# Running the first two token blocks in halves: where the head of an eight-core decoder kernel waits for its loads

## The chip, the cores and the metric

The kernel runs on all 8 cores of one Trainium2 chip. Every core handles one prompt sequence of 2048 tokens, as four blocks of 512, and 128 sample tokens as a fifth block, and reads all the weights for itself. The metric is the time of the slowest core in microseconds (us) on the device. Executions agree within about 0.3% when nothing disturbs them.

Two kinds of disturbed runs occur, whatever the kernel. In slow runs one die, or both, run at a lower granted clock (down to 0.81 here) and the time rises by 28 to 513 us; they are left out. Besides, in some runs one pair of neighbouring cores has a granted clock near 0.982 instead of 0.994, and takes about 27 us longer than the rest; these count as fast runs by the rule used, but 27 us is more than what this study is about. I call a run **clean** when no core is below 0.988, and give for each kernel the median of its clean runs. As a second measure I give the median span of all cores above 0.988, over all its runs.

## The reference, cut to what matters

Two layers. Each begins with half a step of a gated feed-forward network (FFN), then a token mixer, then another such half step and a gated embedding. The change touches the first FFN alone:

```python
def rmsnorm(x, g):
    inv = lax.rsqrt(jnp.mean(x * x, axis=-1, keepdims=True) + NORM_EPS)
    return x * inv * g
def swiglu(h, w_gate_up, w_down):
    gu = h @ w_gate_up                     # (B, S, 2*D_FF), D_FF = 2816 = 22 * 128
    gate, up = gu[..., :D_FF], gu[..., D_FF:]
    return (jax.nn.silu(gate) * up) @ w_down
x = x + 0.5 * swiglu(rmsnorm(x, norm_ffn[i, 0]), w_ffn_gate_up[i, 0], w_ffn_down[i, 0])
```

D_MODEL is 1024, so X of a block of 512 tokens is 8 chunks of 128 x 512 f32: 256 KB a chunk, 2 MB a block. A weight tile ("gu") holds 128 gate and 128 up columns: 1 MB in f32, written as 512 KB of bf16.

## The kernel before

X lies in SBUF, the core's working memory, with the features on its 128 partitions. A recording layer keeps the regions that every instruction reads and writes, and works out the semaphores that each has to wait for. Weights come through a ring, issued by GpSimd; X is issued by SyncE, and every second chunk of block 0 by ScalarE. One unit of the gate and up stage is one weight tile on one block: 16 matmuls of 512 columns, 3.45 us when TensorE runs at full clock. The first FFN starts with "lead" tiles: four tiles run on block 0, then block 1, while blocks 2 to 4 still load. For blocks 0 and 1 the norm's scale is applied after the matmuls, so that they can start on any chunk that has landed.

```python
# the recording layer: the region of an access pattern (X arenas have quads == False)
lo, hi = base + off * es, base + (off + ext) * es      # from the first element to the last
...
if not quads:
    return ((arena, lo, hi),)

# norm of blocks 0 and 1, chunk by chunk
class RawNorm:
    def chunk(self, c):
        dve_ts(H[b][:, c, :], X[b][:, c, :], pcol(self.gname, c), ALU.mult)      # VectorE
        act(sq[:, 0:n], X[b][:, c, :], AF.Square)                               # ScalarE
    def stats(self):        # sum of squares by 8 matmuls with ones, then 1/sqrt on ScalarE

# the loads at the start (cut)
W.pump(1)                                              # weight tile 0
dma("act", PAR[:, :], d_par[:, :], "psem")
for b in range(NB):
    for c in range(8):
        dma("act" if b == 0 and c % 2 else "sp", X[b][:, c, :], ..., f"x{b}_{c}",
            extra=(("wsem2", 0, 16),) if b == 1 and c == 0 else ())    # X1 after weight tile 1
W.extra[1] = (("x0_3", 0, 16),)                        # tiles 1 and 2 after chunk 3 of X0
W.extra[3] = (("x1_2", 0, 16),)                        # tile 3 after chunk 2 of X1
W.extra[4] = tuple((f"x{SB}_{c}", 0, 16) for c in range(8))   # tile 4 and later after X4
W.pump()
...
first = [(0, 0), (1, 0), (2, 0), (0, 1), (1, 1), (2, 1), (3, 0), (3, 1)]   # (tile, block)
advance(ffn(0, 0, "norm_mix0", lead=4, raw=raw, first=first, arrive=arrive))
```

A name such as `wsem2` stands for the landing of a weight tile: `wsem0` is tile 0, `wsem2` tile 1, `wsem8` tile 4. A wait of this sort on an issue is called a gate below.

## Time and profile before

| | before |
|---|---|
| time, median of 3 runs (4 later) | 2630.95 us (2631.64) |
| spans of the cores in the profiled run | 2617.4 to 2623.8 us, clock 0.994 to 0.995 |
| TensorE busy | 98% of the span |
| TensorE idle in the first 60 us of core 3 | 60 - 41.78 = 18.2 us |
| first matmul of block 2, core 3 | 55.45 us |

First the page: its head and the line with the busy time of each engine (engine, us, share of the span, instructions).

```profile
span 2623.8 us, 34956 instructions; the slowest of 8 cores (2617.4 to 2623.8 us)
PE 2569.3 (98%) x14375; PEld 1245.7 (47%) x14375; DVE 1154.5 (44%) x2039; ACT 708.4 (27%) x1257; POOL 168.0 (6%) x254
```

TensorE (PE) has 2569 us of matmuls, and no order removes one. Only its idle time is to be had. The windows view of core 3, the slowest core of this run, says where that lies: each line is one stretch, its length, then each engine's busy time and instructions, the granted clock, the DMA's busy share and GB/s.

```profile
0.00:60.00 60.00, 41.78 (x180) 17.38 (x181) 28.77 (x67) 35.25 (x53) 5.11 (x13) 1.00 0.85 203
60.00:110.00 50.00, 50.00 (x293) 25.18 (x292) 25.62 (x50) 14.05 (x30) 2.12 (x4) 1.00 0.49 84
110.00:500.00 390.00, 390.00 (x2076) 187.80 (x2074) 160.71 (x253) 63.56 (x112) 10.59 (x20) 1.00 0.18 30
```

All the idle time up to 500 us is in the first 60 us. The waits of TensorE up to 85 us (total, times, longest) and its timeline (start, duration, then what ended the idle time before) say what it waits for:

```profile
PE ps L553 <- DMA ring<-wts: 13.8, 3, 12.3
PE ps L553 <- DVE h_50 L523: 1.5, 1, 1.5
PE ps L553 <- DVE h_49 L528: 1.4, 2, 1.1
PE ps L553 <- ACT sq_88 L510: 1.4, 1, 1.4
```

```profile
12.29 5.55 PE L553 MATMUL ps<-h_48,ring 128*128 128x512 bf16 x16 [12.29 <-DMA ring<-wts]
17.68 1.89 PE L553 MATMUL ps<-hid_56,ones 128*128 128x512 bf16 x8
20.88 3.63 PE L553 MATMUL ps<-h_48,ring 128*128 128x512 bf16 x16 [1.31 <-DMA ring<-wts]
24.67 3.63 PE L553 MATMUL ps<-h_48,ring 128*128 128x512 bf16 x16 [0.17 <-DMA ring<-wts]
28.13 1.03 PE L553 MATMUL ps<-h_49,ring 128*128 128x512 bf16 x4
...
55.45 1.90 PE L553 MATMUL ps<-h_50,ring 128*128 128x512 bf16 x8 [1.53 <-DVE h_50 L523]
```

The names h_48 to h_52 are blocks 0 to 4, x_43 to x_47 their X. TensorE starts when tile 0 has landed, runs block 0 on tiles 0 to 2, then block 1 as its chunks come. Of the 18.2 us, 12.3 pass before the first matmul. The rest is in six small waits.

From 8 to 11 us, while all three queues had work, they moved almost the same number of packets, and the weights' packets took most of the time:

```profile
q0 software_dynamic: 74, 0.30, 61.8%
q1 hardware_dynamic: 75, 0.15, 18.1%
q10 hardware_dynamic: 77, 0.16, 16.7%
```

The MB of this view are bytes written: a weight tile counts as 0.52 MB, though 1 MB is read for it.

### The profile page before, as it was taken

The numbers are of one execution on the slowest core, as the hardware profiler recorded it, in microseconds if no ns is written. First come the engines' busy times: TensorE is split into PE (matmuls) and PEld (weight loads), VectorE is DVE, ScalarE is ACT, GpSimd is POOL, SyncE is SP. The second block draws the span as 40 slices with busy tenths as digits, with TensorE's granted clock in tenths as the row PEclk, the third lists the DMA queues.
The fourth block names the chain that finished last, engine by engine and source line by source line (L and its number), as shares of the span: only waits on it lengthen the run. The fifth ranks groups of instructions, "written<-read, shape, count | busy, mean of one in ns | idle before, by whom it ended". The sixth has DMA issues, their size and how long they took to land.

```text
span 2623.8 us, 34956 instructions; the slowest of 8 cores (2617.4 to 2623.8 us)
## 1 busy us (share of the span) xinstructions
PE 2569.3 (98%) x14375; PEld 1245.7 (47%) x14375; DVE 1154.5 (44%) x2039; ACT 708.4 (27%) x1257; POOL 168.0 (6%) x254
## 2 busy tenths in 40 slices
PE   7999999999899999999999999999999999999997
PEld 3544544444454454444444454445444544544443
DVE  5432344755632222258732222267667322222687
ACT  5210112336621001124521001123334210011254
POOL 0000000012300000000000000000005000000000
PEclk9999999999999999999999999999999999999998
DMA  8220321146341123112042031102310320322113
GB/s 199 51 45 1 65 45 25 24 100 120 78 74 33 25 39 54 29 29 50 1 77 41 17 57 33 33 13 42 61 33 8 57 53 17 57 37 41 21 22 137
DMA packets 53311, 127.18 MB, mean 48 GB/s; under 512 B 9504, under 2 KB 24608, under 8 KB 53024
## 3 DMA queue, kind: packets, MB, share of 16 engines
q0 software_dynamic: 23584, 92.55, 20.4%
q1 hardware_dynamic: 28848, 31.29, 4.4%
q8 instruction: 113, 1.85, 0.3%
q10 hardware_dynamic: 720, 1.11, 0.1%
q14 instruction: 46, 0.38, 0.0%
HBM read 196.61 MB, written 10.62 MB: 79 GB/s over the span
## 4 chain that ended last, share of the span: by engine, by line
PE 88%; DVE 5%; ACT 2%; DMA 2%; issue 1%; SPq 1%; POOL 0%; ACTq 0%; DVEq 0%; POOLq 0%
PE ps L553 88%; SPq L577 1%; DMA ring<-wts 1%; ACT L508 1%; DVE h_50 L523 1%; DVE x_46 L523 0%; DVE h_51 L523 0%; DMA x_43<-xT 0%; DMA rr<-u 0%; DVE h_48 L523 0%; DVE h_49 L523 0%; POOL scr_96 L519 0%; DVE x_45 L523 0%; DVE x_43 L523 0%; DVE scr_93 L523 0%
## 5 line engine op out<-in xcount | busy, mean ns | idle before, releaser
L553 PE MATMUL ps<-h_48,ring 128*128 128x512 bf16 x1892 | 429.6, 380 | 14.4 <-DMA ring<-wts 14.4
L553 PE MATMUL ps<-h_51,ring 128*128 128x512 bf16 x1892 | 427.8, 380 | 3.2 <-DVE scr_96 L523 3.0
L553 PE MATMUL ps<-h_49,ring 128*128 128x512 bf16 x1892 | 427.7, 379 | 1.9 <-DVE h_49 L528 1.4
L553 PE MATMUL ps<-h_50,ring 128*128 128x512 bf16 x1892 | 426.2, 379 | 1.5 <-DVE h_50 L523 1.5
L553 PEld LDWEIGHTS ps<-h_51,ring 128*128 128x128 bf16 x1892 | 185.0, 98 | 228.0 <-DVE scr_96 L523 4.0
L553 PEld LDWEIGHTS ps<-h_50,ring 128*128 128x128 bf16 x1892 | 184.7, 98 | 225.3 <-DVE h_50 L523 2.0
L553 PEld LDWEIGHTS ps<-h_49,ring 128*128 128x128 bf16 x1892 | 184.4, 98 | 225.0 <-DVE h_49 L528 3.8
L553 PEld LDWEIGHTS ps<-h_48,ring 128*128 128x128 bf16 x1892 | 181.4, 98 | 220.1 <-issue 14.6
L577 POOL DMA_DIRECT2D ring<-wts x152 | 80.8, 538 | 2048.6 <-PE ps L553 1960.7
L553 PE MATMUL ps<-hid_56,ring 128*128 128x512 bf16 x736 | 163.8, 379 | 0.0
L553 PE MATMUL ps<-hid_54,ring 128*128 128x512 bf16 x736 | 163.7, 379 | 0.0
L553 PE MATMUL ps<-hid_55,ring 128*128 128x512 bf16 x736 | 163.7, 379 | 0.0
L553 PE MATMUL ps<-hid_53,ring 128*128 128x512 bf16 x736 | 162.8, 379 | 0.0
L510 ACT ACTIVATE scr_94<-ps 128x512 f32<-128x512 f32 (+1 forms) x109 | 61.6, 565 | 323.2 <-PE ps L553 322.9
L510 ACT ACTIVATE scr_97<-ps 128x512 f32<-128x512 f32 (+1 forms) x134 | 69.8, 521 | 282.4 <-PE ps L553 274.8
L510 ACT ACTIVATE scr_96<-ps 128x512 f32<-128x512 f32 (+1 forms) x120 | 68.5, 571 | 237.4 <-PE ps L553 235.2
L510 ACT ACTIVATE scr_95<-ps 128x512 f32<-128x512 f32 (+1 forms) x131 | 68.6, 524 | 234.8 <-PE ps L553 234.5
L553 PE MATMUL ps<-h_52,ring 128*128 128x128 bf16 x1892 | 124.5, 221 | 4.6 <-DVE scr_95 L523 3.1
L553 PEld LDWEIGHTS ps<-h_52,ring 128*128 128x128 bf16 x1892 | 115.3, 99 | 27.5 <-DVE scr_95 L523 3.3
L553 PEld LDWEIGHTS ps<-hid_56,ring 128*128 128x128 bf16 x736 | 72.0, 98 | 86.8
L553 PEld LDWEIGHTS ps<-hid_54,ring 128*128 128x128 bf16 x736 | 72.0, 98 | 86.6
L553 PEld LDWEIGHTS ps<-hid_55,ring 128*128 128x128 bf16 x736 | 72.0, 98 | 86.6
(490 smaller groups left out, 2171.8 us busy)
## 6 DMA issues: line engine op xcount, KB each, us to landing
ring<-wts POOLq DMA_DIRECT2D x110, 512.0 KB, 8.4
ring<-wts POOLq DMA_DIRECT2D x40, 768.0 KB, 6.4
rr<-u SPq DMA_DIRECT2D x48, 135.0 KB, 5.3
rr<-u SPq DMA_DIRECT2D x16, 134.8 KB, 3.5
x_44<-xT SPq DMA_DIRECT2D x8, 256.0 KB, 6.2
x_45<-xT SPq DMA_DIRECT2D x8, 256.0 KB, 11.2
x_46<-xT SPq DMA_DIRECT2D x8, 256.0 KB, 11.6
yT<-x_43 SPq DMA_DIRECT2D x8, 256.0 KB, 2.1
```

The lines of the kernel that those rows point to most:

```text
L508: e.preload_act_table_set(tset)
L510: return e.activation(out=out, in_=in_, func=func, **kw)
L523: S.op("dve", lambda e: e.scalar_tensor_tensor(out=out, in0=in0, scalar=scalar, in1=in1, op0=op0, op1=op1), reads=rd, writes=[out])
L553: ins = e.matmul(o_, l, r, start=st, stop=sp)
L577: S.op(eng, lambda e: e.dma_start(out=out, in_=in_), reads=[in_], writes=[out], dma_sem=sem, dma_total=total, extra_deps=extra)
```

## The change

The intent: TensorE should start on 256 tokens of block 0 as soon as those have landed, and likewise in block 1; X of each half loads by itself; a fifth lead tile gives TensorE 6.9 us more work before block 2 is needed. The gates move from the weights to X: weight tiles 0 to 4 are issued at once, X0's second half after its first, X1 after tile 1, X2 and later after tile 4. Shortened:

```diff
-        def chunk(self, c):
+        def chunk(self, c, lo=0, hi=512):
...
-                ensure(("n" if rw is None else "raw", b))
+                for t in (("n", b),) if rw is None else (("raw", b, 0), ("raw", b, 1)):
+                    if not half or t[2] <= half[0]:
+                        ensure(t)
...
-    W.pump(1)
+    def load_x(eng, b, c0, c1, lo=0, hi=None, extra=()):
+        dma(eng, X[b][:, c0:c1, lo:hi], src[:, c0:c1, lo:hi], f"x{b}_{c0}_{lo}", extra=extra)   # (cut)
     dma("act", PAR[:, :], d_par[:, :], "psem")
-    for b in range(NB):
-        for c in range(8):
-            dma("act" if b == 0 and c % 2 else "sp", X[b][:, c, :], d_xT[:, o_:o_ + n], f"x{b}_{c}",
-                extra=(("wsem2", 0, 16),) if b == 1 and c == 0 else ())
-    W.extra[1] = (("x0_3", 0, 16),)
-    W.extra[3] = (("x1_2", 0, 16),)
-    W.extra[4] = tuple((f"x{SB}_{c}", 0, 16) for c in range(8))
+    for c in range(0, 8, 2):
+        load_x("sp", 0, c, c + 2, 0, 256)
+    for c in range(0, 8, 2):
+        load_x("act", 0, c, c + 2, 256, 512, (("x0_6_0", 0, 16),) if c == 0 else ())
+    for lo in (0, 256):
+        for c in (0, 4):
+            load_x("sp", 1, c, c + 4, lo, lo + 256, (("wsem2", 0, 16),) if lo + c == 0 else ())
+    for b in range(2, NB):
+        for c in range(0, 8, 2):
+            load_x("sp", b, c, c + 2, extra=(("wsem8", 0, 16),) if b == 2 and c == 0 else ())
+    W.extra[5] = tuple((f"x{SB}_{c}_0", 0, 16) for c in range(0, 8, 2))
     W.pump()
...
-    first = [(0, 0), (1, 0), (2, 0), (0, 1), (1, 1), (2, 1), (3, 0), (3, 1)]
-    advance(ffn(0, 0, "norm_mix0", lead=4, raw=raw, first=first, arrive=arrive))
+    first = [(0, 0, 0), (0, 0, 1), (1, 0), (2, 0), (0, 1, 0), (1, 1, 0), (2, 1, 0), (3, 0), (0, 1, 1), (1, 1, 1), (2, 1, 1)]
+    first += [(3, 1), (4, 0), (4, 1)]          # (tile, block, half)
+    advance(ffn(0, 0, "norm_mix0", lead=5, raw=raw, first=first, arrive=arrive))
```

A transfer of a half now covers two chunks (four in block 1) and 256 of the 512 columns of each.

More of the change, by code (lines that the diff above doesn't have):

```diff
@@ L735, in __init__, with stats @@
             self.rs = RSB[b]
-        def chunk(self, c):
-            n, b = self.n, self.b
-            sq = HID[SB - 1 - b][:, c, :]
-            dve_ts(H[b][:, c, :], X[b][:, c, :], pcol(self.gname, c), ALU.mult)
-            act(sq[:, 0:n], X[b][:, c, :], AF.Square)
-        def stats(self):
-            n = self.n
+        def chunk(self, c, lo=0, hi=512):
+            b = self.b
+            dve_ts(H[b][:, c, lo:hi], X[b][:, c, lo:hi], pcol(self.gname, c), ALU.mult)
+            act(HID[SB - 1 - b][:, c, lo:hi], X[b][:, c, lo:hi], AF.Square)
+        def stats(self, lo=0, hi=512):
             pb = bank()
-            mm(pb[:, 0:n], [(ONES[:, :], HID[SB - 1 - self.b][:, c, 0:n]) for c in range(8)])
-            act(self.rs[:, 0:n], pb[:, 0:n], AF.Abs_reciprocal_sqrt, bias=NORM_EPS)
+            mm(pb[:, lo:hi], [(ONES[:, :], HID[SB - 1 - self.b][:, c, lo:hi]) for c in range(8)])
+            act(self.rs[:, lo:hi], pb[:, lo:hi], AF.Abs_reciprocal_sqrt, bias=NORM_EPS)
             bfree(pb)
@@ L752, in lead_order @@
         for b in range(NB):
-            out += [(t, b) for t in range(min(lead, nt)) if (t, b) not in out]
+            out += [(t, b) for t in range(min(lead, nt)) if (t, b) not in [x[:2] for x in out]]
         for t in range(lead, nt):
@@ L756, in lead_order @@
         last = {}
-        for i, (t, b) in enumerate(out):
-            last[t] = i
+        for i, x in enumerate(out):
+            last[x[0]] = i
         return out, last
@@ L818, in ffn @@
             order, last = lead_order(len(part), lead if pi == 0 else 0, first if pi == 0 else None)
-            for oi, (j, b) in enumerate(order):
-                n = BLK[b]
+            for oi, (j, b, *half) in enumerate(order):
+                lo, hi = (256 * half[0], 256 * half[0] + 256) if half else (0, BLK[b])
+                n = hi - lo
                 rw = raw[b] if b < len(raw) else None
-                ensure(("n" if rw is None else "raw", b))
+                for t in (("n", b),) if rw is None else (("raw", b, 0), ("raw", b, 1)):
+                    if not half or t[2] <= half[0]:
+                        ensure(t)
                 key = ("gu", l, f, part[j])
@@ L825, in ffn, with tail @@
                 pg, pu = bank(), bank()
-                pe_t[0] = max(pe_t[0], arrive.get((pi, j, b), 0.0))
+                pe_t[0] = max(pe_t[0], arrive.get((pi, j, b, *half), 0.0))
                 if rw is not None and pi == 0 and j == 0:
                     for k in range(8):
-                        mm_ops([(pg[:, 0:n], wt[:, k, 0:128], H[b][:, k, :], k == 0, k == 7),
-                                (pu[:, 0:n], wt[:, k, 128:256], H[b][:, k, :], k == 0, k == 7)])
+                        mm_ops([(pg[:, 0:n], wt[:, k, 0:128], H[b][:, k, lo:hi], k == 0, k == 7),
+                                (pu[:, 0:n], wt[:, k, 128:256], H[b][:, k, lo:hi], k == 0, k == 7)])
                         pe_t[0] += 2 * (n + 6.5) / 2400.0
-                    rw.stats()
+                    rw.stats(lo, hi)
                 else:
-                    mm(pg[:, 0:n], [(wt[:, k, 0:128], H[b][:, k, :]) for k in range(8)])
-                    mm(pu[:, 0:n], [(wt[:, k, 128:256], H[b][:, k, :]) for k in range(8)])
+                    mm(pg[:, 0:n], [(wt[:, k, 0:128], H[b][:, k, lo:hi]) for k in range(8)])
+                    mm(pu[:, 0:n], [(wt[:, k, 128:256], H[b][:, k, lo:hi]) for k in range(8)])
                 sg = scr()
                 if rw is not None:
-                    dve_tt(sg[:, 0:n], pg[:, 0:n], rw.rs[:, 0:n], ALU.mult)
+                    rs = rw.rs[:, lo:hi]
+                    dve_tt(sg[:, 0:n], pg[:, 0:n], rs, ALU.mult)
                     bfree(pg)
                     act(sg[:, 0:n], sg[:, 0:n], AF.Silu)
-                    def tail(b=b, j=j, n=n, sg=sg, pu=pu, rs=rw.rs):
-                        dve_tt(sg[:, 0:n], sg[:, 0:n], rs[:, 0:n], ALU.mult)
-                        dve_tt(HID[b][:, j, :], pu[:, 0:n], sg[:, 0:n], ALU.mult)
+                    def tail(b=b, j=j, n=n, lo=lo, hi=hi, sg=sg, pu=pu, rs=rs):
+                        dve_tt(sg[:, 0:n], sg[:, 0:n], rs, ALU.mult)
+                        dve_tt(HID[b][:, j, lo:hi], pu[:, 0:n], sg[:, 0:n], ALU.mult)
                         bfree(pu)
                         sfree(sg)
-                    defer(1.5, tail)
+                    defer(1.5 if n == 512 else 0.8, tail)
                 else:
@@ L1215, in ple @@
             W.done(("pleg", l, ch))
-    W.pump(1)
-    dma("act", PAR[:, :], d_par[:, :], "psem")
-    for b in range(NB):
-        n = BLK[b]
-        for c in range(8):
-            o_ = 8 * BOFF[b] + c * n
-            dma("act" if b == 0 and c % 2 else "sp", X[b][:, c, :], d_xT[:, o_:o_ + n], f"x{b}_{c}",
-                extra=(("wsem2", 0, 16),) if b == 1 and c == 0 else ())
-    W.extra[1] = (("x0_3", 0, 16),)
-    W.extra[3] = (("x1_2", 0, 16),)
-    W.extra[4] = tuple((f"x{SB}_{c}", 0, 16) for c in range(8))
+    def load_x(eng, b, c0, c1, lo=0, hi=None, extra=()):
+        n = BLK[b]
+        hi = hi or n
+        src = kview(d_xT[:, 8 * BOFF[b]:8 * (BOFF[b] + n)], 8)
+        dma(eng, X[b][:, c0:c1, lo:hi], src[:, c0:c1, lo:hi], f"x{b}_{c0}_{lo}", extra=extra)
+    dma("act", PAR[:, :], d_par[:, :], "psem")
+    for c in range(0, 8, 2):
[9 more added lines that the diff above has]
+    W.extra[5] = tuple((f"x{SB}_{c}_0", 0, 16) for c in range(0, 8, 2))
     W.pump()
@@ L1230, in build_program @@
     for c in range(8):
-        raw[0].chunk(c)
+        raw[0].chunk(c, 0, 256)
         if c == 0:
@@ L1244, in build_program @@
     for c in range(8):
-        at_time(19.5 + 0.87 * c, lambda c=c: raw[1].chunk(c), ("raw", 1))
+        at_time(11.0 + 0.1 * c, lambda c=c: raw[0].chunk(c, 256, 512), ("raw", 0, 1))
+    for h in range(2):
+        for c in range(8):
+            at_time((23.5, 30.5)[h] + 0.1 * c, lambda c=c, h=h: raw[1].chunk(c, 256 * h, 256 * h + 256), ("raw", 1, h))
     n0 = [Norm(b, "norm_ffn00", "pe" if b < SB else "dve") for b in range(NB)]
@@ L1249, in build_program @@
         for mo in range(8):
-            at_time((27.0, 37.0, 47.0)[b - 2] + (0.8, 1.0, 0.5)[b - 2] * mo,
+            at_time((38.0, 45.0, 52.0)[b - 2] + (0.8, 1.0, 0.5)[b - 2] * mo,
                     lambda b=b, mo=mo: n0[b].chunk(mo, 0.0), ("n", b))
-    first = [(0, 0), (1, 0), (2, 0), (0, 1), (1, 1), (2, 1), (3, 0), (3, 1)]
-    arrive = {(0, 1, 0): 15.5, (0, 2, 0): 18.5, (0, 3, 0): 28.5}
-    advance(ffn(0, 0, "norm_mix0", lead=4, raw=raw, first=first, arrive=arrive))
+    first = [(0, 0, 0), (0, 0, 1), (1, 0), (2, 0), (0, 1, 0), (1, 1, 0), (2, 1, 0), (3, 0), (0, 1, 1), (1, 1, 1), (2, 1, 1)]
+    first += [(3, 1), (4, 0), (4, 1)]
+    arrive = {(0, 0, 0, 1): 13.5, (0, 1, 0): 17.2, (0, 2, 0): 22.5, (0, 0, 1, 0): 26.0, (0, 0, 1, 1): 33.0}
+    advance(ffn(0, 0, "norm_mix0", lead=5, raw=raw, first=first, arrive=arrive))
     for l in range(2):
```

## The prediction

> What bounds the kernel. TensorE: the page gives it 98% of the 2623.8 us span, and no matmul is removed, so only its idle time can be won. In the head of the slowest core (core 3, windows view) TensorE is busy 37.8 of the first 56.0 us: 18.2 us idle; from 56 to 300 us it is busy throughout. By the waits and the timeline the idle time is: 12.3 before the first matmul (the first weight tile lands 10.6 us after issue, sharing the DMA engines with all of X block 0), 1.3 and 0.2 for weight tiles 1 and 2 (issued only after a chunk of X0; the DMA idles from about 14.7 to 17 us), about 1.6 for h_49, 1.4 for a square of X2 (ScalarE), 1.5 for h_50 (VectorE). The first 16 matmuls take 5.2 us, where warm ones take 3.45; the Trainium skill, "TensorE: Matmul & The Clock Gate", section "Part 1: The HAM clock gate", says the first busy stretch runs at half clock, and their spacing of 0.43 us against 0.216 agrees. The head is limited by DMA: busy share 0.9 to 1.0 nearly all of 3 to 49 us, reading 250 to 290 GB/s (estimate: 12.5 MB by 50 us).
>
> What the change does.
> 1. Until the first half of X0 has landed, 1 MB of X instead of 2 competes with the weights. The skill, "DMA: Bandwidth & Descriptors", section "Queues, rings and completion order", says each engine goes round-robin over its queues; here three queues took about equal engine time. With two, I estimate first tile and first half at 10 to 10.5 us, 2 us earlier.
> 2. Weight tiles 1 to 4 are queued at once: the DMA hole goes. But X0's second half now competes with tiles 1 and 2, landing near 18 us; TensorE idles 3 to 5 us between the halves.
> 3. X1 in halves: three 256-token units begin at about 26 us.
> 4. A fifth lead tile puts two more units (6.9 us of matmuls) in front of block 2, while X2 loads. X2 starts only after tile 4, near 36 to 39 us; X ends at about 53 us.
> 5. Costs: more small VectorE and ScalarE instructions (0.69 and 0.63 us at 512), up to four more table loads of 1.28 us on ScalarE, which was busy 8.9 of 10 us from 36 to 46 us. Packets of 512 B and 2 KB cost about 29 and 90 ns here, so 1 KB packets should add under 10% of DMA time.
>
> Sum. Before, block 2 starts at 55.5 us after 8 lead units. After: first matmul at 10.3, ten units and the squares' sums done by 57 to 60. Two units and two sums more are worth 7.3 us, the later start of block 2 costs 2 to 4.5. Gain 3 to 5.5 us on slow cores, all critical, since TensorE never idles from then to 500 us. Later stages keep their order (only buffer numbers rotate). I predict 2626.5 us, range 2622.5 to 2630.5; chances: faster by over 2% 0.01, within 2% 0.98, slower 0.01.
>
> What would show it. First matmul near 10.3 us; TensorE idle 13 to 15.5 us in the first 60 us; no DMA hole near 15 us; block 2's first matmul at 57 to 60 us; no new idle time between 60 and 500 us.
>
> What would make it wrong. ScalarE's in-order queue holds the first half's squares behind the issue of X0's second half; a late second half of X1 holds silus behind its squares, and so banks; the first tile lands no earlier because its own transfer bounds it; X2 lands so late that the sums stall TensorE. Then the gain shrinks to zero.

## More of the kernel before

One more view matters, the DMA queues from 6 to 12 us, while tile 0 loads beside X0: packets, MB, share of the 16 engines' time. q0 carries the weights, q1 what SyncE issues, q10 what ScalarE issues.

```profile
q0 software_dynamic: 143, 0.52, 54.8%
q10 hardware_dynamic: 229, 0.42, 22.5%
q1 hardware_dynamic: 201, 0.36, 21.2%
```

While it streams, the weight queue has more than half of the engines' time. I had read this view over a longer stretch, from 2 to 12 us, where the shares are 33.5, 33.8 and 24.9%, because the weights' first packets move only at about 6 us.

## The result, and the profile after

| | before | after |
|---|---|---|
| time, median of 4 runs | 2631.64 us (2630.5 to 2632.41) | 2652.76 us (2650.03 to 2654.89) |
| ratio of fast runs | | 1.008 (95%: 1.0063 to 1.0098) |
| repetition on another chip, clean runs | 2626.9 us (9) | 2648.4 us (4) |
| repetition, median span of undisturbed cores | 2621.3 us | 2643.1 us |
| TensorE idle in the first 110 us, core 3 | 18.2 us | 37.5 us |
| first matmul of block 2, core 3 | 55.45 us | 82.94 us |

A ratio is the mean time of one kernel's fast runs over that of the other's fast runs of the same rounds, so it is not quite the ratio of the medians. Time went up by 21 us, 0.8%, where I had expected it to fall by 5. In the first profile the upper die's clock was 0.991 against 0.995, worth some microseconds more there; in the clean runs of the repetition all cores had 0.993 to 0.996 and the difference was the same 21 us, so the clock is not its cause.

The views of core 3 again, first the page's head and busy line (that page is of core 7, the slowest), then the windows:

```profile
span 2651.9 us, 35167 instructions; the slowest of 8 cores (2638.0 to 2651.9 us)
PE 2580.7 (97%) x14455; PEld 1256.5 (47%) x14455; DVE 1157.4 (44%) x2067; ACT 716.7 (27%) x1283; POOL 167.6 (6%) x254
```

```profile
0.00:60.00 60.00, 26.46 (x164) 16.14 (x165) 18.74 (x70) 22.29 (x48) 5.12 (x13) 1.00 0.84 201
60.00:110.00 50.00, 46.07 (x238) 22.69 (x236) 31.80 (x61) 30.72 (x52) 0.00 (x0) 1.00 0.21 34
110.00:500.00 390.00, 390.00 (x2135) 190.21 (x2134) 153.48 (x242) 62.02 (x112) 12.71 (x24) 1.00 0.24 37
```

All of the loss is in the head: 33.5 us idle in the first 60 and 3.9 in the next 50, none from 110 to 500 us. The DMA is as busy as before (0.84 against 0.85) and moves as much (201 GB/s against 203): the same bytes arrive, in another order. TensorE's waits and its timeline:

```profile
PE ps L553 <- DVE h_48 L528: 22.3, 2, 21.6
PE ps L553 <- DMA ring<-wts: 10.1, 1, 10.1
PE ps L553 <- ACT sq_88 L510: 3.2, 1, 3.2
```

```profile
10.12 0.58 PE L553 MATMUL ps<-h_48,ring 128*128 128x256 bf16 x2 [10.12 <-DMA ring<-wts]
32.33 3.31 PE L553 MATMUL ps<-h_48,ring 128*128 128x256 bf16 x14 [21.63 <-DVE h_48 L528]
...
38.55 1.70 PE L553 MATMUL ps<-h_48,ring 128*128 128x256 bf16 x12 [0.65 <-DVE h_48 L528]
...
42.28 7.07 PE L553 MATMUL ps<-h_48,ring 128*128 128x512 bf16 x32
...
82.94 7.29 PE L553 MATMUL ps<-h_50,ring 128*128 128x512 bf16 x33 [0.70 <-DVE h_50 L523]
```

The first matmul comes 2.2 us earlier, as forecast. But after the two matmuls of chunk 0, TensorE waits 21.6 us for chunk 1 of the first half. VectorE, which makes that chunk, and the issues on ScalarE's and SyncE's queues (timelines of those three engines):

```profile
5.29 0.35 DVE L528 TENSOR_SCALAR h_48<-x_43,par 128x256 bf16<-128x256 f32 x1 [5.29 <-DMA x_43<-xT]
31.92 0.61 DVE L528 TENSOR_SCALAR h_48<-x_43,par 128x256 bf16<-128x256 f32 x2 [26.14 <-DMA x_43<-xT]
```

```profile
22.58 2.88 ACTq L577 DMA_DIRECT2D x_43<-xT  x4
```

```profile
14.02 18.62 SPq L577 DMA_DIRECT2D x_44<-xT  x4
```

Two things are odd. ScalarE may issue the second half of X0 only when the last transfer of the first half has landed, and does so at 22.58 us. I had put that at 10.5. And although the first half is there at 22.58, VectorE starts its chunk 1 only at 31.92. Also the four issues of X1 (x_44) take 18.6 us on SyncE's queue: it waits in the midst of them. The DMA queues from 10 to 22 us explain the first:

```profile
q0 software_dynamic: 464, 1.70, 83.7%
q1 hardware_dynamic: 465, 0.45, 16.7%
```

The weights had 464 packets and X 465: the DMA engines take one packet from each queue in turn. A weight packet occupies an engine for 83.7% x 12 us x 16 / 464 = 346 ns, a packet of half a chunk (1 KB) for 69 ns. So while the weights stream, X gets a sixth of the time.

The order of instructions explains the second. The waits that the recording layer gave VectorE's chunks (not a profile; names are x, block, first chunk, first column):

```
1 L528 TensorScalarPtr h_48<-x_43,par 128x256 [waits psem,x0_0_0]
3 L528 TensorScalarPtr h_48<-x_43,par 128x256 [waits x0_0_256]
4 L528 TensorScalarPtr h_48<-x_43,par 128x256 [waits x0_2_0]
5 L528 TensorScalarPtr h_48<-x_43,par 128x256 [waits x0_2_256]
```

Chunk 1 of the *first* half waits for `x0_0_256`, the *second* half of chunks 0 and 1. The layer takes a pattern with gaps as one range from its first byte to its last. The second half of chunks 0 and 1 then "covers" the first half of chunk 1, which lies between its two pieces. By the same rule X1's second half waits for its first, which is the wait on SyncE's queue.

### The profile page after: what moved, and what is told of

It reads as the page before. It is cut to its first block, busy times and chain, and to the rows that moved or that the text cites. A ratio compares the mean times of both kernels' runs of the same rounds, so it can differ in the third digit from the quotient of the medians.

```text
span 2651.9 us, 35167 instructions; the slowest of 8 cores (2638.0 to 2651.9 us)
## 1 busy us (share of the span) xinstructions
PE 2580.7 (97%) x14455; PEld 1256.5 (47%) x14455; DVE 1157.4 (44%) x2067; ACT 716.7 (27%) x1283; POOL 167.6 (6%) x254
## 4 chain that ended last, share of the span: by engine, by line
PE 90%; DVE 4%; DMA 2%; ACT 2%; issue 1%; SPq 1%; POOL 0%; ACTq 0%; DVEq 0%; POOLq 0%
PE ps L553 90%; DMA x_43<-xT 1%; ACT L508 1%; DMA ring<-wts 1%; SPq L577 1%; DVE h_48 L523 0%; DVE x_46 L523 0%; DMA xscr_69<-st_sc 0%; DVE h_49 L523 0%; DVE x_45 L523 0%; DVE v L523 0%; DMA rr<-u 0%; DVE h_50 L523 0%; DVE h_51 L523 0%; ACT h_51 L510 0%
## 5 line engine op out<-in xcount | busy, mean ns | idle before, releaser
L553 PE MATMUL ps<-h_48,ring 128*128 128x512 bf16 (+1 forms) x1908 | 432.8, 380 | 33.6 <-DVE h_48 L528 22.1
L553 PE MATMUL ps<-h_49,ring 128*128 128x512 bf16 (+1 forms) x1940 | 432.0, 377 | 0.5 <-DVE scr_94 L523 0.5
L553 PE MATMUL ps<-h_51,ring 128*128 128x512 bf16 x1892 | 428.4, 381 | 2.6 <-DVE scr_95 L523 2.5
L553 PE MATMUL ps<-h_50,ring 128*128 128x512 bf16 x1892 | 429.3, 381 | 0.8 <-DVE h_50 L523 0.7
L553 PE MATMUL ps<-hid_54,ring 128*128 128x512 bf16 x736 | 164.2, 380 | 0.0
L553 PE MATMUL ps<-hid_55,ring 128*128 128x512 bf16 x736 | 163.9, 379 | 0.0
L553 PE MATMUL ps<-hid_56,ring 128*128 128x512 bf16 x736 | 163.7, 379 | 0.0
L553 PE MATMUL ps<-hid_53,ring 128*128 128x512 bf16 x736 | 162.8, 379 | 0.0
## 6 DMA issues: line engine op xcount, KB each, us to landing
x_44<-xT SPq DMA_DIRECT2D x4, 512.0 KB, 10.5
x_46<-xT SPq DMA_DIRECT2D x4, 512.0 KB, 12.6
```

The costliest lines, as they stand in the source:

```text
L553: ins = e.matmul(o_, l, r, start=st, stop=sp)
```

## The experiments

Two theories at the start. **Theory D**: the false dependency is the loss; the first half is not used before the second has landed. **Theory Q**: the five weight tiles, issued at once, take the DMA from X, packet by packet. Fourteen kernels ran; all were correct. All differences are against the kernel before in the same submission; the first four share a chip, the next four, the next three (the same chip as the four before, measured later), then one, then two.

| run | clean runs, us (number) | before, us | difference | undisturbed cores, difference | ratio of fast runs (95%) |
|---|---|---|---|---|---|
| e1 exact tracking | 2654.8 (2) | 2626.6 | +28.2 | +23.9 | 1.0082 (0.9974 to 1.019) |
| e2 tile 1 gated on X0 | 2645.3 (2) | 2626.6 | +18.7 | +16.9 | 1.008 (0.9972 to 1.0188) |
| e3 both | 2639.2 (4) | 2626.6 | +12.6 | +12.1 | 1.0024 (0.9961 to 1.0087) |
| e4 before, tiles 1 to 3 ungated | 2630.8 (1) | 2626.6 | +4.2 | +5.8 | 1.006 (0.9952 to 1.0169) |
| e5 the change again | 2648.4 (4) | 2626.9 | +21.5 | +21.8 | 1.0115 (1.0074 to 1.0157) |
| e6 first half of X0 on two queues | 2645.4 (3) | 2626.9 | +18.5 | +18.9 | 1.0097 (1.0057 to 1.0137) |
| e7 weights first | 2634.9 (1) | 2626.9 | +8.0 | +7.6 | 1.0106 (1.0068 to 1.0145) |
| e8 early weights | 2629.1 (3) | 2626.9 | +2.2 | +1.3 | 1.0057 (1.0015 to 1.0099) |
| e9 exact, X1 gated on X0 | 2643.3 (3) | 2628.6 | +14.7 | +14.7 | 1.0053 (1.0034 to 1.0072) |
| e10 fifth tile alone | 2627.1 (5) | 2628.6 | -1.5 | -0.9 | 0.9994 (0.9981 to 1.0007) |
| e11 two tiles early | 2631.8 (5) | 2628.6 | +3.2 | +4.1 | 1.0011 (0.9998 to 1.0024) |
| e12 halves, old gates | 2639.8 (3) | 2628.6 | +11.2 | +11.1 | 1.0042 (1.0022 to 1.0062) |
| e13 halves, mended gates | 2630.3 (4) | 2629.2 | +1.1 | +1.9 | 1.0004 (0.9991 to 1.0017) |
| e14 fifth tile, gate earlier | 2626.8 (5) | 2629.2 | -2.4 | -1.1 | 0.999 (0.9977 to 1.0003) |

The ratios and their intervals hold the runs with a disturbed pair of cores too, on either side, which is why some are wide and do not match the columns beside them. The first submission was on a disturbed chip (four of the seven runs of the kernel before were slow, or had a slow pair), so for e1, e2 and e4 I rest on the undisturbed cores and on the traces. Times below are read from core 4 of each run, unless another core is named.

### e1: exact tracking

```diff
         if not quads:
+            if arena[0] == "x" and len(pat) == 3 and pat[1][1] > 1 and pat[2][1] < pat[1][0]:
+                w, st = pat[2][1] * es, pat[1][0] * es
+                return tuple((arena, lo + i * st, lo + i * st + w) for i in range(pat[1][1]))
             return ((arena, lo, hi),)
```

> The changed kernel, but the recording layer tracks a strided X transfer chunk by chunk instead of as one range, so the first-half chunks of X0 and X1 no longer wait for the second-half transfers. Theory D (the false dependency is the whole loss): the first 16 matmuls finish by 15 us and the time falls to 2632 us or less. Theory Q (the five ungated weight tiles starve X0, one packet each in turn): the first half still lands only at about 22 us and the second at about 31 us. Both together: first unit done near 23 us, tile 1 starts near 33 us instead of 42 us, 2640 to 2645 us.

Measured: +23.9 us, no gain at all. The first half's matmuls now follow its landings, but the last of them still come at 24.5 us, so the half lands as late as before. The second half got later: its last chunk's matmuls start at 43.3 us (in e5 they were over by 39.5 us), tile 1 at 45.8 us, and at 50.5 us on the slowest core. So D as the whole cause is dead. The DMA queues of this run from 30 to 42 us show why the second half was late:

```profile
q1 hardware_dynamic: 1211, 3.02, 75.3%
q10 hardware_dynamic: 913, 0.88, 25.1%
```

q10 is X0's second half, in packets of 1 KB. q1 is X1 and X2, whose packets average 2.5 KB. The false dependency had held SyncE's queue back; without it X1 and X2 got in front of what TensorE was waiting for. It had worked as a gate.

### e2: weight tile 1 gated on X0's second half

```diff
+    W.extra[1] = (("x0_6_256", 0, 16),)
```

> The changed kernel, but weight tile 1 is issued only when X0's second half has landed; the false dependency stays. Theory D: chunk 1 still waits for the second half, so most of the loss stays, above 2645 us. Theory Q: X0 is complete near 15 us, tile 1 starts near 21 us, X1 then shares one packet each with tiles 2 to 4 and comes late (about 37 us with the dependency): 2632 to 2638 us.

Measured: +16.9 us, a fifth of the loss of the change gone; theory D had said most stays, and most stayed, but not by its reasoning. X0 was complete near 18 us instead of 33, and the two tiles after the first began at 26.1 us instead of 41.5 us. Then block 1 came late: its first half's chunk 0 at 36.5, the others from 42.6 us, since X1 now competed with tiles 2 to 4, and had the false dependency too. What is gained in block 0 is lost in block 1. I had expected 2632 to 2638 us on a chip where the kernel before takes some 5 us more than here; it was 2645.3.

### e3: both repairs

> Both repairs at once. First half landed near 10 us, second near 15 us, tile 1 at about 21 us, first half of X1 at about 31 us. If the two causes are the whole loss, block 2 starts near 60 us and the time is 2626 to 2630 us, as I had predicted for the change itself. If something else costs too (scalar engine, fifth lead tile), it stays above 2634 us.

Measured: +12.1 us, so something else costs as well. The first half is at work at 11.6 us as wanted. The rest is gates in a row. X0's second half is issued after the first has landed, and lands near 20 us, not 15. Tile 1 is issued after that and lands at 27.4 us; TensorE waits 3.1 us for it. X1 is issued after tile 1, against tiles 2 to 4, and TensorE waits twice for its chunks (2.9 and 1.4 us) at 40 and 43 us. From 12 to 20 us the DMA is busy only 0.54 of the time, as the windows show; the first half's sums of squares also wait 2.1 us for ScalarE, whose queue was busy issuing transfers, as the prediction had feared. And the wait cost more than itself:

```profile
12.00:20.00 8.00, 4.66 (x27) 3.05 (x25) 2.77 (x26) 5.26 (x13) 0.28 (x1) 1.00 0.54 132
...
28.00:40.00 12.00, 9.15 (x31) 3.42 (x29) 2.47 (x5) 1.03 (x3) 0.00 (x0) 0.78 1.00 186
```

The granted clock of the second stretch is 0.78 on average, and 0.50 from 28 to 32 us. The 32 matmuls of tiles 1 and 2 took 9.8 us instead of 7.1. The Trainium skill, "TensorE: Matmul & The Clock Gate", section "Part 1: The HAM clock gate", says that about 3.4 us of idleness lets the clock fall to a half; here the fall followed a wait of 3.1 us. The length of one wait does not decide it in these runs. In e4 the half clock (0.50 from 20 to 28 us) followed a wait of 2.5 us. On core 4 of e7 it came (0.50 from 54 to 56 us) after a wait of 1.4 us with shorter gaps behind it, TensorE being busy for 1.3 us of 50 to 53 us. And on core 5 of e8 a wait of 3.2 us left the next 32 matmuls at full speed, in 7.08 us. What does decide it is not shown.

### e4: the kernel before with tiles 1 to 3 ungated

```diff
-    W.extra[1] = (("x0_3", 0, 16),)
-    W.extra[3] = (("x1_2", 0, 16),)
```

> The kernel before (whole chunks of X0, no halves, no false dependency), with weight tiles 1 to 3 issued at once. Theory Q: X0's last chunk lands at 19 to 23 us instead of 14.6 us, since weights and each X queue take turns packet by packet; the later tiles and X1 come earlier, so the time moves little, 2628 to 2636 us. Theory D alone: X0 lands about when it did, and the hole in the DMA near 15 us is gone, 2626 us or less.

Measured: +5.8 us. X0's last chunks are used at 23.1 us instead of 16 to 17; theory Q's number came true in a kernel that has no halves and no false dependency. The later tiles and X1 came without waits, which gave most of it back: ungated weights alone cost 4 to 6 us, not 21. Part of these is the half clock after its waits for chunks: the eight sums of squares at 24 us took 3.6 us instead of 1.9.

### e5: the change again

> The changed kernel unaltered, beside the other runs on their chip, and as a repetition: 2645 to 2655 us in fast runs, cores' spans about 2638 to 2650 us, chunk 1 of the first half at 31 to 33 us, tile 1's first matmuls at 41 to 44 us.

Measured: +21.8 us, chunk 1 at 31.7 us, tile 1 at 41.5 us: the result repeats.

### e6: the first half of X0 on two queues

```diff
-        load_x("sp", 0, c, c + 2, 0, 256)
+        load_x("act" if c % 4 else "sp", 0, c, c + 2, 0, 256)
```

> The changed kernel, with the four transfers of X0's first half issued alternately from two engines, so that X has two queues against the weights' one; all else stays, the false dependency too. Theory Q in its packet form (each DMA engine takes one packet from each queue in turn, and a weight packet lasts about 350 ns against 70 ns): X0's first half lands near 15 us instead of 22.6 us, everything after it moves up by 5 to 8 us, cores' spans fall by 5 to 8 us. If the queues share by time or bytes, two X queues get two thirds instead of a half, and the first half lands near 10 us. If bandwidth of the memory is the limit whatever the queues, nothing moves.

Measured: ScalarE had issued the last transfer of X0's second half by 18.8 to 20.7 us on the eight cores, against 25.2 to 26.6 us in e5. As issuing four takes some 2 us, the first half landed near 17.5 us instead of 23.5: 6 us earlier by the choice of the issuing engine alone. A fixed share of time or of bytes would have given 10 us by my reckoning, and the view below excludes both: 79.8% of the time and 0.73 MB for the weights, 17.3% and 0.20 MB for X. But X had two turns against one only for a while. Its lead was won in the first 8 us: 838 packets of X0 had moved by then (534 on q1 and 448 on q10, less 144 of the parameters), against 551 in e5. Part of that came before the weights' first packets, at 4 to 6 us, and how much is due to turns is not separated. After 8 us only ScalarE's queue still held X, and it went one for one with the weights. From 8 to 14 us:

```profile
q0 software_dynamic: 198, 0.73, 79.8%
q10 hardware_dynamic: 199, 0.20, 17.3%
q1 hardware_dynamic: 10, 0.01, 0.5%
```

The span fell by only 2.9 us, less than I had said. X0's second half, issued by 19.2 us, moved only 65 packets before 23 us, and from 23 to 29 us it took turns with X1's first half, 847 packets against 848, so that tile 1 starts at 39.1 us instead of 41.5.

### e7: weights first

The change with exact tracking, X0's halves one behind the other on one queue without a gate, tile 1 gated on the first half, X1 whole and ungated, and all five lead tiles on block 0 before block 1.

```diff
+    for lo in (0, 256):
+        for c in range(0, 8, 2):
+            load_x("sp", 0, c, c + 2, lo, lo + 256)
+    for b in range(1, NB):
+        for c in range(0, 8, 2):
+            load_x("sp", b, c, c + 2)
+    W.extra[1] = (("x0_6_0", 0, 16),)
...
+    first = [(0, 0, 0), (0, 0, 1), (1, 0), (2, 0), (3, 0), (4, 0)]
```

> A version built on both theories: exact tracking; X0 in halves on one queue without a gate between the halves; weight tile 1 gated only on the first half; no halves in X1; block 0 runs all five lead tiles first, in the order in which the weights stream, then block 1. First half near 10.5 us, second near 15 us, tiles 1 to 4 every 3.5 to 5 us, block 1 from about 35 us, block 2 from 57 to 60 us. If Q and the gaps between gates are the causes, 3 to 6 us faster than the kernel before on the same chip; if the scalar engine or the fifth tile cost, slower.

Measured: +7.6 us, a miss. X0 is complete by 20 us, but tile 1, issued at 14.8, landed only at 26.0 us. After the issue the weights' queue moved a single packet before 19 us, while X1, which had followed X0 on its queue at once, had the DMA to itself; why the weights' first packets came so late is not shown (in the kernel before, tile 1's came some 2.5 us after its issue). Then the two queues took turns: 184 packets of weights and 188 of X1 from 20 to 26 us, with 68% of the time for the weights. So the tile was late by its start and by sharing, not starved as X0 had been. TensorE waited 4.0 us for it, and ran on slowly after that: 46 matmuls in 11.6 us.

### e8 and e11: early weights, without halves

Both are the kernel before with the fifth lead tile (edit under e10, but with the squares at 28, 38 and 49 us). e8 gates tile 1 on chunk 0 of X0 and tile 2 on chunk 5; e11 leaves the second gate out.

```diff
-    W.extra[1] = (("x0_3", 0, 16),)
+    W.extra[1] = (("x0_0", 0, 16),)
+    W.extra[2] = (("x0_5", 0, 16),)      # e8 only
```

> The kernel before without halves, with the fifth lead tile alone from the change, weight tile 1 queued once the first chunk of X0 has landed and tile 2 once the sixth has, and the squares of blocks 2 to 4 placed a little later. X0 complete near 16 us, tile 1 near 17 us, X1 complete near 27 us, no wait of TensorE for sq or h_50 over 1 us: 3 to 6 us faster than before. If the fifth lead tile costs by itself (its load delays X2 and X3), no gain.

> The early-weights version, with tile 2 queued right behind tile 1 (after X0's first chunk) instead of after its sixth, which had made TensorE wait 3.2 us and fall to the half clock again. X0 complete near 18 us, tile 1 at 21 us, tile 2 without a wait, X1 complete near 28 us, block 2 at about 57 us after ten units: 4 to 6 us faster than before, clean runs 2621 to 2624 us. If it is X1 that then waits behind the weights, no faster than before.

Measured: +1.3 us and +4.1 us; both misses. In e8 tile 2 was issued at 18 us and landed at 27.8, with 3.2 us of waiting and, on core 4, half the clock after it. In e11 there is no wait for a tile, but X0's last chunk comes at 23.4 us (core 5) instead of the 18 I had expected: from 12 to 16 us the three queues moved 118, 117 and 117 packets there. In these runs every tile that starts earlier pushes X0 back by more.

### e9: exact tracking, X1 gated on X0's second half

```diff
-            load_x("sp", 1, c, c + 4, lo, lo + 256, (("wsem2", 0, 16),) if lo + c == 0 else ())
+            load_x("sp", 1, c, c + 4, lo, lo + 256, (("x0_6_256", 0, 16),) if lo + c == 0 else ())
```

> The exact-tracking run again, but X1 is gated on X0's second half instead of on weight tile 1. In the earlier run, removing the false dependency let X1 and X2 (on their own queue, larger packets) in before X0's second half, which landed only at about 47 us. If that is why removing the dependency gained nothing, the second half now lands at 30 to 34 us, tile 1 starts at 33 to 36 us instead of about 50 us, and the cores' spans fall to about 2630 to 2636 us. If the dependency costs nothing by itself, they stay at 2640 us or more.

Measured: +14.7 us where e1 had +23.9 and the change +21.8. The second half is used from 32.3 us and tile 1 starts at 37.4 us (36 to 37 us on cores 2 and 5), instead of 45.8 and 41.5 us. So the two edits together, exact tracking and X1's gate, are worth about 7 us against the change; the gate without exact tracking was not run, so they are not told apart here. A pair on one chip that differs in the dependency alone is e2 and e3: +16.9 against +12.1, so that with tile 1 gated its removal is worth 4.8 us. It was a real cost, and theory D was right in kind and wrong in size; the span's 2638 us is a little above what I had expected.

### e10: the fifth lead tile alone

```diff
+    W.extra[4] = (("x1_7", 0, 16),)
+    W.extra[5] = tuple((f"x{SB}_{c}", 0, 16) for c in range(8))
-    first = [..., (3, 0), (3, 1)]                    # lead=4
+    first = [..., (3, 0), (3, 1), (4, 0), (4, 1)]    # lead=5
-    at_time((27.0, 37.0, 47.0)[b - 2] + ...)         # when the squares of blocks 2 to 4 are placed
+    at_time((29.0, 41.0, 51.0)[b - 2] + ...)
```

> The kernel before with the fifth lead tile alone (its load gated on X1's last chunk, squares of blocks 2 to 4 placed 2 to 4 us later). DMA before X2 grows by 3.5 us. The waits for sq_88 (1.4 us) and h_50 (1.5 us) should go: 1 to 3 us faster, clean runs 2624 to 2626 us. If the later X2 and X3 make TensorE wait at their squares, no gain or 1 to 2 us slower.

Measured: 1.5 us faster in clean runs, 0.9 us by the cores; the wait for h_50 is gone, that for squares is 0.9 us in two pieces. The ratio's interval (0.9981 to 1.0007) includes 1. So the fifth tile shows no cost, and is perhaps worth a microsecond.

### e12 and e13: all the halves, with gates like those before

e12 has exact tracking, all halves and the fifth tile. X0's halves follow one another on two queues without a gate; tile 1 waits for a chunk of X0's second half, tile 3 for part of X1's second half, tile 4 for all of it, X2 to X4 for nothing. e13 moves two gates and one entry of the order.

```diff
-    W.extra[1] = (("x0_2_256", 0, 16),)
+    W.extra[1] = (("wsem0", 0, 16),)
-    W.extra[3] = (("x1_0_256", 0, 16),)
+    W.extra[3] = (("x1_0_0", 0, 16),)
-    ..., (2, 1, 0), (3, 0), (0, 1, 1), (1, 1, 1), (2, 1, 1)]
+    ..., (2, 1, 0), (0, 1, 1), (1, 1, 1), (2, 1, 1), (3, 0)]
```

> The change with all its halves and the fifth lead tile, but with exact tracking and the gates of the kernel before: X0's halves one behind the other on two queues without a gate, weight tile 1 after a chunk of X0's second half, tile 3 after part of X1, tile 4 after all of it, X2 to X4 ungated. If the loss lies wholly in the gates and the false dependency, X0's second half lands at 15 to 16 us, tile 1 starts near 20 us, the halves of X1 near 27 and 33 us, and the clean runs lie within 3 us of the kernel before (0 to 3 us faster is what I hope for). If halves cost by themselves (smaller packets, more instructions on ScalarE), it stays 5 us or more slower.

> The last run with tile 1 gated on tile 0's landing, tile 3 on the first transfer of X1, and the second half of X1 used by tiles 0 to 2 before tile 3 is needed. No wait of over 2 us for a weight tile after the first. If halves cost nothing by themselves, clean runs within 2 us of the kernel before; if they do (smaller packets lose turns to the weights, six more table loads and 256-token instructions on ScalarE), they stay 3 us or more above it, and the extra idle time of TensorE lies at chunks of h_48 and h_49 or at squares.

Measured: e12 +11.1 us. I had gated tile 3 too late: it was issued at 33.4 us, and TensorE waited 7.2 us for it at 44.7. e13, with that mended, +1.9 us by the cores and +1.1 us in clean runs (ratio 1.0004). Its waits up to 85 us:

```profile
PE ps L556 <- DMA ring<-wts: 12.6, 1, 12.6
PE ps L556 <- ACT hid L513: 2.0, 3, 1.1
PE ps L556 <- ACT sq L513: 1.9, 1, 1.9
PE ps L556 <- DVE h L526: 1.1, 1, 1.1
PE ps L556 <- DVE h L531: 1.0, 2, 0.6
```

No wait for a weight after the first. The halves do their work: chunks of X cost 1.0 us of waiting. What they win there they lose on ScalarE: 2.0 us of waits for its squares (hid), which come behind another half's instructions in its queue, and which the kernel before doesn't have. The first matmul is not earlier than before. Against the kernel before, the halves with the fifth tile are thus within 2 us. But the fairer partner is e14 below: it has the fifth tile and the same gate on tile 1, without halves. Against it e13 is slower by 3.4 us in clean runs (2630.27 against 2626.83) and by 3.0 by the cores. The gate of tile 3 and the order of the units differ too; with that said, the halves gain nothing, and seem to cost some 3 us.

### e14: the fifth tile, with tile 1's gate on tile 0

```diff
-    W.extra[1] = (("x0_3", 0, 16),)       # e10 with this
+    W.extra[1] = (("wsem0", 0, 16),)
```

> The fifth lead tile alone, with tile 1 gated on tile 0's landing (about 13 us) instead of on chunk 3 of X0 (about 14 us). The hole in the DMA near 15 us shrinks by about 1 us: 1 to 3 us faster than the kernel before, 2625.5 to 2627.5 us if that reads 2628.5 us. If X0's last chunks are then late, no gain over the fifth tile alone.

Measured: 2.4 us faster than before in clean runs (2626.8 against 2629.2), 1.1 us by the cores; ratio 0.999 (0.9977 to 1.0003). It is the best version that I found, but with an interval that reaches 1 it can't be called proven. Whether it beats e10 is open: their differences to the kernel before come from different chips.

## Why the prediction was wrong

**What held.** TensorE bounds the kernel and only the head matters: yes; from 110 to 500 us it is busy throughout in both kernels. First matmul near 10.3 us: 10.1 us on core 3, 10.1 to 11.5 on all eight; but this is luck in part, as I got it from an equal share of the time, while the weights had 85.9% of it at 8 to 10 us. The fifth tile is no loss: e10. More table loads and small instructions do not matter much: e13, though ScalarE's queue costs about 2 us there (2.0 us of waits for its squares). The hole in the DMA near 15 us went, as said.

**The step that failed.** It is step 1: "here three queues took about equal engine time. With two, I estimate first tile and first half at 10 to 10.5 us". The tile came then, the half did not: it landed at 22.6 us. The Trainium skill, "DMA: Bandwidth & Descriptors", section "Queues, rings and completion order", says that each DMA engine goes round its queues "at *packet* granularity". I cited the place and turned it into equal time. The trace agrees with the page to the packet (464 against 465), and the packets lasted 346 and 69 ns, a ratio of five. The change halves the width of X's packets, takes X0's first half from two queues to one, and ungates five tiles: all three take turns, or bytes per turn, from X. My "equal engine time" was a mean over 10 us in which the weight queue was empty for the first four. e4 shows this step's mechanism apart from the rest; e6 shows that the choice of queues alone moves the landing by 6 us, though not by turns alone.

**What I did not look at.** The second omission follows: the false dependency. The waits of each instruction were to be had without a run, and I looked only at the order of matmuls. The prediction took it for granted that a half is free when it has landed. It holds TensorE from 22.6 to 32.3 us. e9 against the change puts its worth, and that of the better gate for X1, at 7 us; e3 against e2 puts its worth alone at 4.8 us where tile 1 is gated; e1 shows that taking it out of the change alone gives nothing, because it had also kept X1 and X2 off the DMA.

**What the sum lacked.** Step 2 has X0's second half "landing near 18 us". It was issued only at 22.6 us, by a gate on the first half, and ended near 33. Each gate costs the transfer's landing, the issue and the start of the next transfer, and during that the DMA partly idles: busy 0.54 of 12 to 20 us in e3. With both faults repaired, e3 still lost 12 us to gates in series, to X1 behind tiles 2 to 4, and to the half clock after a wait of 3.1 us. With the gates of before, mended, e13 was within 2 us of the kernel before. Thus nearly all of the loss lies in the order of the transfers and in the dependency, and none that shows in the fifth tile; the halves themselves seem to cost some 3 us (e13 against e14), which the sum had as a gain.

**Where the forecast gain went.** Block 2's first matmul was to come at 57 to 60 us and came at 82.94 us; before, it was at 55.45. Of the 27.5 us between, 7.3 are work put in front of it; 20.2 are lost. The two waits for chunks of h_48, 22.3 us together, less the 2.2 us of the earlier start, make 20.1 of that; the other waits (5.9 us before, 5.1 after) and 0.9 us more of slow matmuls nearly cancel.

**What stays open.** How the 21.8 us divide between starvation and dependency can't be said as a sum: the two repairs do not add (e1 +23.9, e2 +16.9, e3 +12.1), and the traces of e1 and e2 show another transfer late each time: X0's second half in one, X1 in the other. The change with X1's gate alone was not run. Whether e10 or e14 really beat the kernel before needs more runs than these.

## What to carry to other kernels

When transfers queue up, count turns, not bytes: the DMA engines here took one packet from every queue in turn, so a stream with small packets on one queue gets a small share beside one with large packets, and every "issue it at once" takes time from what is needed first. Before you believe that a part of a load can be used early, read which semaphore each consumer waits for: a tracker that takes a strided pattern as one range makes it wait for its neighbour. And repair in pairs: here removing a false wait gained nothing until another transfer that it had held back was gated on purpose.

## What the Trainium skill lacked or had wrong

- "DMA: Bandwidth & Descriptors", section "Queues, rings and completion order": right about turns by packet, but it does not say that the share of time then goes with how long a packet lasts. Here 464 packets of weights (1.70 MB written, so 3.7 KB and 346 ns each) had 83.7% and 465 packets of X (1 KB, 69 ns each) 16.7%.
- "DMA: Bandwidth & Descriptors", section "Issuing engines are not separate DMA queues": it says that issuing from several engines saves only the sequencer's time. For the total that may hold; for one stream against another it does not. Issuing half of the same transfers from a second engine brought X0's first half in about 6 us earlier, near 17.5 us instead of 23.5 (e6).
- "TensorE: Matmul & The Clock Gate", section "Part 1: The HAM clock gate": about 3.4 us of idleness is given for the fall to half clock. Here the half clock (0.50) followed waits of 3.1 us (e3: 32 matmuls in 9.8 us instead of 7.1), 2.5 us (e4) and, with shorter gaps behind it, 1.4 us (e7, core 4), and a wait of 3.2 us did not bring it on core 5 of e8.
- No page that I read mentions that a pair of neighbouring cores can run a whole execution at a granted clock of 0.982 instead of 0.994, about 27 us longer of 2625, in otherwise fast runs; three of e4's four runs were such.
